# Seven block products instead of eight in the projections of the second 1024 tokens

## The chip, the cores and the metric

The kernel runs on one core of a Trainium2 chip. The metric is the device time of one execution in microseconds, as the median of several runs. The engines are TensorE (PE; its weight loads are shown apart as PEld), VectorE (DVE), ScalarE (ACT), GpSimd (POOL) and SyncE (SP), which issues nearly all transfers.

## The reference

One layer on x of 2048 tokens by 1024. `xn = RMSNorm(x)`, `proj = xn @ w_in`, and `proj` is split into the queries, keys, values and gates of two mixers (qa, ka, va, ga of 512 columns each; qb, gb of 512; kb, vb of 64), an indexer (iq, ik, iw) and two merge gates (za, zb of 1024 each). Mixer A is chunked attention with a relative bias, mixer B attends to the 256 keys per query that the indexer scores highest. Then

```python
merged = gate_a * (ya @ w_branch_a) + gate_b * (yb @ w_branch_b)
h = h + merged @ w_out
return rms_norm(h, final_norm_gain)
```

All data are float32. The change concerns only `xn @ w_in` for the columns qa, ka, ga, qb, gb, za and zb, and the tokens 1024 to 2047.

## The kernel before, in words

**Products.** Each float32 operand is split into a high part, rounded to TensorE's float32 format, and a low part, the rest. `mm3` (line 194) forms a product of 128 by 128 by 512 with three matmuls: high by high, high by low, low by high. The normalized input stands in `xh` and `xl` (lines 150, 151), two slots of [128, 8, 512]: 8 slices of 128 input features, 512 tokens.

**Projections.** `UNITS` (line 63) lists 20 units of 256 columns: zb 4, za 4, gb 2, ga 2, qb 2, va 2, ka 2, qa 2. `steps` (lines 714 to 718) is the order of work: all units on token groups 0 and 1 (the first 1024 tokens), where the last two units go on to groups 2 and 3, then the other units on groups 2 and 3. `prep` (line 173) loads and splits one unit's weights (ScalarE the high part, GpSimd the low part), one unit ahead, in two buffers; each unit's weights are loaded once for each pass. The main loop (line 1177) runs each step: two column tiles of 8 x 3 = 24 matmuls of 512 columns (for va, token tiles of 24 matmuls of 288 columns), each into one of three PSUM banks, and `evac` (line 665) applies the gate's function or the split and stores the result to DRAM. `norm_again` (line 1167) replaces the input of groups 0 and 1 by that of groups 2 and 3 in the same slots.

**What runs beside it.** After each column tile the loop calls `tick(1)` (line 1152; 0.5 for va). While the indexer's scores (`logits`, line 442) and the search for the 256 best keys (`search`, line 477) have work left, a tick lets them put `PUMP` = 3850 ns of counted work into the program (`pump`, line 622). Once they are done and `OPEN` = 138 ticks have passed (of 160), `open_early` (line 731) closes the search's memory, and each tick puts two rounds of attention (`attention`, line 1122) into the program, up to a pause before the seventh unit. After the projections the attention goes on, followed by the output product.

**Order.** The source gives each instruction a priority by its place in the program; a planner then lays down, ahead of time, a fixed order for every engine and for the SP queue: of the instructions that it takes to be ready, the earliest in the program first. On the chip each engine runs its list in that order. Tiles of a pool with one tag share its buffers, so a write waits for the last reader of the tile before.

## Time and profile before

| | us |
|---|---|
| median of 3 runs | 2084.61 (2083.42 to 2085.93) |
| profiled execution | 2085.01 |
| its span, first to last instruction | 2083.2 |

The profile shows one execution. A busy time is the time in which an engine had at least one instruction under way; matmuls are pipelined, so the time from start to start in a full stretch, not the duration of one, tells what a matmul costs. The times on the left of rows are counted from the start of the span.

### The profile page before, as it was taken

How to read it: one execution, taken by the hardware profiler on the slowest of the kernel's cores; microseconds unless marked ns; L12 is line 12 of the kernel's file. 1: busy time of each engine (PE TensorE's matmuls, PEld its weight loads, DVE VectorE, ACT ScalarE, POOL GpSimd, SP SyncE). 2: the span in 40 equal slices, each digit the busy share in tenths (PEclk: the TensorE clock that was granted, in tenths of full speed). 3: DMA queues.
4: the chain of work that ended last, by engine and by line, in shares of the span. 5: the costliest groups of instructions: out<-in, count | busy, mean ns of one | idle time of the engine just before them, and what ended most of it. 6: DMA issues, size and time to landing. Idle time of an engine off the chain costs nothing. (4 is left out here: it accounts for less than half of the span.)

```text
span 2083.2 us, 33122 instructions
## 1 busy us (share of the span) xinstructions
PE 2023.5 (97%) x10858; PEld 1719.6 (83%) x10858; DVE 1316.1 (63%) x3380; ACT 1196.3 (57%) x2372; POOL 688.3 (33%) x753
## 2 busy tenths in 40 slices
PE   8799999999999999999999999999999999999998
PEld 7578887889888888887987888888898888887886
DVE  6747958786987845002325668766885688865444
ACT  5455655555456454223436778866896698873221
POOL 2122223221202211122323455445444644442410
PEclk9899999999999999999999999999999999999999
DMA  9473344464443333226557774666346632145642
GB/s 354 155 223 117 134 143 143 139 205 146 157 170 137 117 112 105 86 91 197 186 185 224 222 215 148 180 189 207 114 136 190 215 119 65 62 137 187 213 141 91
DMA packets 237378, 331.12 MB, mean 159 GB/s; under 512 B 29328, under 2 KB 119824, under 8 KB 237072
## 3 DMA queue, kind: packets, MB, share of 16 engines
q1 hardware_dynamic: 237200, 328.96, 48.9%
q8 instruction: 86, 1.41, 0.3%
q14 instruction: 92, 0.75, 0.1%
HBM read 222.47 MB, written 106.40 MB: 158 GB/s over the span
## 5 line engine op out<-in xcount | busy, mean ns | idle before, releaser
L199 PE MATMUL acc<-xh,wt 128*128 128x512 f32 x2304 | 738.8, 395 | 2.6 <-DVE e L318 2.6
L199 PEld LDWEIGHTS acc<-xh,wt 128*128 128x128 f32 x2304 | 431.9, 188 | 101.1 <-DVE e L318 2.8
L199 PE MATMUL acc<-xl,wt 128*128 128x512 f32 x1152 | 452.9, 393 | 0.0
L191 POOL TENSOR_TENSOR wt<-wst,wt 128x512 fp32r<-128x512 f32 (+1 forms) x172 | 202.2, 1192 | 634.1 <-ACT wt L190 625.1
L199 PEld LDWEIGHTS acc<-xl,wt 128*128 128x128 f32 x1152 | 216.7, 188 | 48.8
L807 POOL TENSOR_TENSOR ptl<-pf,pth 128x512 fp32r<-128x512 f32 (+1 forms) x144 | 179.4, 1246 | 214.9 <-ACT pf L803 157.5
L467 DVE SCALAR_TENSOR_TENSOR sc<-lg,iw,sc 128x512 f32<-128x512 f32 (+2 forms) x266 | 179.2, 680 | 81.0 <-ACT lg L462 72.1
L810 DVE TENSOR_TENSOR ptl<-pt,pth 128x512 fp32r<-128x512 f32 (+1 forms) x288 | 187.5, 660 | 53.0 <-ACT pth L809 51.8
L965 PE MATMUL s<-kBt,qsB 128*128 128x512 f32 (+3 forms) x640 | 188.3, 384 | 2.3 <-issue 2.0
L462 ACT ACTIVATE lg<-lg 128x512 f32<-128x512 f32 (+2 forms) x304 | 150.9, 525 | 53.5 <-PE lg L460 52.4
L809 ACT ACTIVATE pth<-pt 128x512 fp32r<-128x512 f32 (+1 forms) x288 | 161.2, 579 | 27.4 <-PE pt L982 13.8
L982 PE MATMUL pt<-ident,P 128*128 128x128 f32 x1088 | 167.1, 273 | 2.1 <-DVE ptl L810 0.8
L968 ACT ACTIVATE P<-P,mx 128x128 f32<-128x128 f32 (+15 forms) x128 | 154.6, 1209 | 18.2 <-DVE mx L786 17.5
L990 PE MATMUL O<-pth,vBt 128*128 128x256 f32 x544 | 148.1, 290 | 2.1 <-DVE yb L1000 1.5
L990 PE MATMUL O<-ptl,vBt 128*128 128x256 f32 x544 | 147.2, 296 | 1.6 <-POOL ptl L807 1.1
L786 DVE CUSTOM_DVE_ANT_0 P<-s,mk,mx 128x512 f32<-128x512 f32 (+2 forms) x192 | 125.2, 652 | 34.3 <-PE s L965 28.3
L190 ACT ACTIVATE wt<-wst 128x512 fp32r<-128x512 f32 (+1 forms) x172 | 92.7, 575 | 81.0 <-DMA wst<-wP 78.5
L982 PEld LDWEIGHTS pt<-ident,P 128*128 128x128 f32 x1088 | 128.4, 140 | 11.4 <-ACT pf L803 2.1
L1028 POOL TENSOR_TENSOR dw<-dst,dw 128x512 fp32r<-128x512 f32 x64 | 82.6, 1291 | 116.2 <-ACT dw L1027 102.1
L965 PEld LDWEIGHTS s<-kBt,qsB 128*128 128x128 f32 x640 | 103.1, 191 | 14.8 <-DVE mx L786 5.1
L990 PEld LDWEIGHTS O<-pth,vBt 128*128 128x128 f32 x544 | 102.9, 189 | 10.7 <-ACT pth L809 2.4
L860 ACT ACTIVATE P<-P,mx 128x640 f32<-128x640 f32 (+4 forms) x128 | 98.1, 767 | 23.2 <-DVE mx L786 22.7
(247 smaller groups left out, 3958.1 us busy)
## 6 DMA issues: line engine op xcount, KB each, us to landing
wst<-wP SPq DMA_DIRECT2D x132, 256.0 KB
qs<-qA SPq DMA_DIRECT2D x128, 128.0 KB
kk<-kA SPq DMA_DIRECT2D x56, 256.0 KB
vs<-vA SPq DMA_DIRECT2D x56, 256.0 KB
bias<-biasD SPq DMA_DIRECT2D x32, 320.0 KB
xrow<-x SPq DMA_DIRECT2D x16, 512.0 KB
sBD<-ef SPq DMA_DIRECT2D x32, 256.0 KB
sAD<-ef SPq DMA_DIRECT2D x32, 256.0 KB
```

The lines of the kernel that those rows point to most:

```text
L191: nc.gpsimd.tensor_tensor(wt[:, 1, k:k + n, c * 128:(c + 1) * 128], st, f32(hi), op=OP.subtract)
L199: nc.tensor.matmul(acc, a, b, start=(i == 0), stop=(i == n - 1))
L462: nc.scalar.activation(lg, lg, AF.Relu)
L467: nc.vector.scalar_tensor_tensor(o_, lg, wv, o_, op0=OP.mult, op1=OP.add)
L786: nc.vector.tensor_tensor_reduce(dst, ps_, add, 1.0, FMAX if first else mx, OP.add, OP.min, accum_out=mx)
L807: nc.gpsimd.tensor_tensor(lo, pf, f32(hi), op=OP.subtract)
L809: nc.scalar.activation(hi, src, AF.Copy)
L810: nc.vector.tensor_tensor(lo, src, f32(hi), op=OP.subtract)
L965: nc.tensor.matmul(s_ps[:, :w], q[:, h, :], kBt[:, m, a:a + w], start=(m == 0), stop=(m == 1))
L968: nc.scalar.activation(P[:, e, :n], P[:, e, :n], AF.Exp, bias=mx[:, e:e + 1], scale=-1.0, accum_out=st["sum"][:, (u % 2) * 2 + e:(u % 2) * ...
L982: nc.tensor.transpose(pt[:, k, e, :], P[:, e, (kt + k) * 128:(kt + k + 1) * 128], ident)
L990: nc.tensor.matmul(o_, vBt[:, kt + k, :], src[:, k, :], start=(kt + k == 0 and n_ == 0), stop=(kt + k == b and n_ == 1), skip_group_check= ...
```

## The change

For 18 units (all but va) the second pass takes the 1024 tokens as two blocks of 512 (groups 2 and 3), the 1024 input features as two blocks of 512 (`A11`, `A12` of group 2, `A21`, `A22` of group 3), and a unit's 256 columns as two of 128. The eight block products are replaced by seven of 4 x 3 = 12 matmuls, by Strassen's scheme, with block sums of the input (in place of the old blocks) and of the weights.

The work is cut in two halves over all units. In the first (`prep_one`, `first_half`), each unit does four products with A11, A21 (by then A11 - A21), A12 and A22 (as loaded), evacuates one finished block, and stores three partial sums to DRAM (`qD`). Between the halves `combine_pe` forms two more block sums on TensorE, with plus or minus the identity as weights; the first and the last sum use `combine` (GpSimd, VectorE, ScalarE). In the second half (`prep_two`, `load_sums`, `part`) each unit does the other three products, adds the sums that it loads from DRAM, and evacuates three blocks. A unit's weights are loaded whole for the first half and three quarters for the second, in rows of 512 bytes; the block sums of weights are made on GpSimd (`TPE`) and their low parts on VectorE (`LOE`). The input block A11 and the first half's weights give up their memory to the second half's weights and sums. The units go in the order `QUADS`. The constants `OPEN` and `PUMP` change; a product of the new kind counts half a tick, so that the program has 151 ticks in place of 160. The order of the last steps of the first pass is turned (group 1 before 0, and 3 before 2), so that group 3 is in place first.

In `evac` the last buffer can be given by the caller (`own`, the sum's own tile), and for qb the two half operations come before the whole one. The core of the diff:

```diff
-OPEN = 138
+OPEN = 142
...
-PUMP = 3850
+PUMP = 4300
...
+QUADS = "qb zb zb qb zb zb ka za za za za ka gb gb qa ga ga qa"
+QB, CTB, WSB = 1, 2, 5
+W2AT = (2, 0)
+TPE, LOE = "gpsimd", "vector"
...
+    qD = [scratch(f"qD{u}", [3, 128, 512]) for u in range(len(UNITS))]
...
+    a_st = phase_p.enter_context(ExitStack())
+    apool = a_st.enter_context(pool("xA"))
+    parts = {(s, h, z): (apool if s + h == 0 else xpool).tile([128, 4, 512], F32R, name=f"x{z}{s}{h}")
+             for s in range(2) for h in range(2) for z in "hl"}
...
+    def mm3(acc, pairs, first=True, last=True):
...
-    steps = [(u, g) for u in range(nu - 2) for g in (0, 1)]
-    steps += [(a_, 0), (b_, 0), (a_, 1), (b_, 1), (a_, 2), (b_, 2), (a_, 3), (b_, 3)]
-    kinds = ("zb", "za", "gb", "ga", "qb", "va", "ka")
-    second = [u for k in kinds for u in range(nu - 2) if UNITS[u][0] == k]
-    steps += [(u, g) for u in second for g in (2, 3)]
-    runs = list(range(nu)) + second
-    last = {}
-    for i, (u, g) in enumerate(steps):
-        last[u if i < 2 * nu + 4 else nu + second.index(u)] = i
+    of = {k: [u for u in range(nu) if UNITS[u][0] == k] for k in dict(UNITS)}
+    va = of["va"]
+    left = {k: list(of[k]) for k in of}
+    quads = [left[k].pop(0) for k in QUADS.split()]
+    rest = []
+    jobs = [("std", u, u, g) for u in range(nu - 2) for g in (0, 1)]
+    jobs += [("std", u, u, g) for g in (1, 0) for u in (a_, b_)]
+    jobs += [("std", nu + u, u, g) for u in rest for g in (3, 2)]
+    jobs += [("std", nu + u, u, g) for g in (3, 2) for u in va]
+    turned = max(i for i, j_ in enumerate(jobs) if j_[3] == 3)
+    jobs += [("one", 2 * nu + u, u, 0) for u in quads]
+    runs = list(dict.fromkeys(j_[1] for j_ in jobs))
...
+    def combine(dst, a, b, op, k):
+        (ah, al), (bh, bl), (dh, dl) = a(k), b(k), dst(k)
+        t, t2 = (evl.tile([128, 512], F32, name="ct", tag="ct", bufs=CTB) for _ in range(2))
+        nc.gpsimd.tensor_tensor(t, f32(ah), f32(bh), op=op)
+        nc.vector.tensor_tensor(t2, f32(al), f32(bl), op=op)
+        nc.vector.tensor_tensor(t, t, t2, op=OP.add)
+        nc.scalar.activation(dh, t, AF.Copy)
+        nc.vector.tensor_tensor(dl, t, f32(dh), op=OP.subtract)
...
+    def combine_pe(dst, a, b, z, k, free):
+        n = (count_["acc"] + 1 + (k % 2 if free == 2 else 0)) % 3
+        acc = (psp, psp, psz)[n].tile([128, 512], F32, name="cm", tag=f"acc{n}")
+        for i, (w, x_) in enumerate(((0, a(k)[0]), (0, a(k)[1]), (z, b(k)[0]), (z, b(k)[1]))):
+            nc.tensor.matmul(acc, signs(w), x_, start=(i == 0), stop=(i == 3))
+        dh, dl = dst(k)
+        nc.scalar.activation(dh, acc, AF.Copy)
+        nc.vector.tensor_tensor(dl, acc, f32(dh), op=OP.subtract)
...
+    def split_w(W, st, k):
+        nc.scalar.activation(W[:, 0, :, k], st, AF.Copy)
+        getattr(nc, LOE).tensor_tensor(W[:, 1, :, k], st, f32(W[:, 0, :, k]), op=OP.subtract)
+    def prep_one(u, at):
+        wt = wpool.tile([128, 2, KT, WT], F32R, name="wt", tag="wt")
+        W = blocks_of(wt, 4)
+        e = getattr(nc, TPE)
+        for k in range(4):
+            st = evl.tile([128, 4, 128], F32, name="wst", tag="wst", bufs=stage[-1][2])
+            for c in range(2):
+                nc.sync.dma_start(st[:, 2 * c:2 * c + 2], io["wP"][u, c, :, k::4, :])
+            e.tensor_tensor(st[:, 2], st[:, 3], st[:, 2], op=OP.subtract)
+            e.tensor_tensor(st[:, 3], st[:, 2], st[:, 0], op=OP.add)
+            e.tensor_tensor(st[:, 3], st[:, 1], st[:, 3], op=OP.subtract)
+            split_w(W, st, k)
+        wcur[at] = W
+    def product(acc, W, b, x_, first, last):
+        mm3(acc, [((W[:, 0, b, k], W[:, 1, b, k]), x_(k)) for k in range(4)], first, last)
+    def first_half(u, W):
         kind, c2 = UNITS[u]
+        a, b = next_acc(5), next_acc(5)
+        p1, s, d = (evl.tile([128, 512], F32, name=f"q{z}", tag=f"q{z}", bufs=QB) for z in range(3))
+        product(a, W, 0, A11, True, False)
+        nc.scalar.activation(p1, a, AF.Copy)
+        nc.sync.dma_start(qD[u][0], p1)
+        yield
+        product(b, W, 2, A21, True, False)
+        nc.vector.tensor_tensor(s, b, p1, op=OP.add)
+        nc.sync.dma_start(qD[u][1], s)
+        yield
+        product(a, W, 1, A12, False, True)
+        evac(kind, c2 * 2, 2, a)
+        yield
+        product(b, W, 3, A22, False, True)
+        nc.vector.tensor_tensor(d, b, p1, op=OP.add)
+        nc.sync.dma_start(qD[u][2], d)
+        yield
...
+    for i, (how, r_, u, g) in enumerate(jobs):
+        kind, c2 = UNITS[u]
+        wt, s_ = wcur[r_], SLOT[g]
+        if how == "one":
+            for n, _ in enumerate(first_half(u, wt)):
+                if u == quads[-1] and n == 1:
+                    for k in range(4):
+                        combine_pe(A21, A22, A21, 1, k, 1)
+                tick(0.5)
...
+        if i == turned:
+            again += [lambda k=k: combine(A21, A11, A21, OP.subtract, k) for k in range(4)]
...
+    w_st.close()
+    second = {}
+    def prep_two(q):
+        u = quads[q]
+        wt = w2.tile([128, 2, 3, 4, 128], F32R, name="wt2", tag="wt2", bufs=3)
+        W = [wt[:, :, z] for z in range(3)]
+        e = getattr(nc, TPE)
+        for k in range(4):
+            if (q, k) < W2AT:
+                st = evl.tile([128, 4, 128], F32, name="wst", tag="wst", bufs=stage[-1][2])[:, 0:3]
+            else:
+                st = w2.tile([128, 3, 128], F32, name="wst2", tag="wst2", bufs=4)
+            nc.sync.dma_start(st[:, 0:1], io["wP"][u, 0, :, k:k + 1, :])
+            nc.sync.dma_start(st[:, 1:3], io["wP"][u, 1, :, k::4, :])
+            e.tensor_tensor(st[:, 1], st[:, 1], st[:, 0], op=OP.subtract)
+            e.tensor_tensor(st[:, 0], st[:, 2], st[:, 1], op=OP.subtract)
+            split_w(wt, st, k)
+        second.setdefault(q, [None, None, None])[0] = W
+    def load_sums(q):
+        second.setdefault(q, [None, None, None])[1] = [w2.tile([128, 512], F32R, name="part", tag=f"p{z}", bufs=2) for z in range(3)]
+        for z in range(3):
+            nc.sync.dma_start(f32(second[q][1][z]), qD[quads[q]][(2, 1, 0)[z]])
+    def part(q, z):
+        u = quads[q]
+        kind, c2 = UNITS[u]
+        W, sums, acc = second[q]
+        if z == 0:
+            acc = second[q][2] = next_acc(5)
+        mm3(acc, [((W[z][:, 0, k], W[z][:, 1, k]), (A21, A22, A12)[z](k)) for k in range(4)], z == 0, z == 2)
+        s = sums[z]
+        nc.vector.tensor_tensor(f32(s), acc, f32(s), op=OP.add)
+        evac(kind, c2 * 2 + (z > 0), 2 if z == 2 else 3, f32(s), own=s)
+        tick(0.5)
+    nq = len(quads)
+    for k in range(4):
+        combine_pe(A22, A21, A11, 0, k, 2)
+    a_st.close()
+    w2 = phase_p.enter_context(pool("w2"))
+    for q in range(2):
+        load_sums(q)
+    for q in range(2):
+        prep_two(q)
+    part(0, 0)
+    for k in range(4):
+        combine(A12, A12, A21, OP.subtract, k)
+    for q in range(nq + 1):
+        if q < nq:
+            if q + 2 < nq:
+                prep_two(q + 2)
+            if q:
+                part(q, 0)
+        if q:
+            part(q - 1, 2)
+            if 1 < q + 1 < nq:
+                load_sums(q + 1)
+        if q < nq:
+            part(q, 1)
```

## Rows read from the trace of the kernel before

**Rows 1.** The page's engine line, and three lines of its 40 equal slices (52 us each; busy share in tenths; DMA is the share of the 16 DMA engines):

```profile
PE 2023.5 (97%) x10858; PEld 1719.6 (83%) x10858; DVE 1316.1 (63%) x3380; ACT 1196.3 (57%) x2372; POOL 688.3 (33%) x753
...
PE   8799999999999999999999999999999999999998
...
DVE  6747958786987845002325668766885688865444
...
DMA  9473344464443333226557774666346632145642
```

**Rows 2.** Stretches of the second pass of the projections and of what follows it. Columns: from:to, length, then busy us (and instructions) of PE, PEld, DVE, ACT and POOL, the granted clock, the DMA share and GB/s; the stretch 950 to 1010 lies within 930 to 1105:

```profile
640.00:830.00 190.00, 190.00 (x823) 154.07 (x822) 128.21 (x301) 103.92 (x158) 46.67 (x36) 1.00 0.35 122
830.00:930.00 100.00, 100.00 (x433) 81.05 (x432) 0.00 (x0) 21.13 (x37) 20.34 (x16) 1.00 0.26 90
930.00:1105.00 175.00, 166.57 (x938) 145.56 (x937) 50.73 (x136) 65.15 (x175) 47.51 (x53) 0.99 0.58 180
950.00:1010.00 60.00, 52.45 (x301) 44.89 (x300) 16.23 (x47) 26.25 (x71) 19.36 (x24) 1.00 0.74 225
1105.00:1120.00 15.00, 11.59 (x66) 9.65 (x65) 7.32 (x28) 10.04 (x28) 4.83 (x5) 0.87 0.87 258
```

**Rows 3.** The same columns for a stretch of 50 us in which TensorE runs projection matmuls alone:

```profile
850.00:900.00 50.00, 50.00 (x218) 40.50 (x217) 0.00 (x0) 9.57 (x17) 10.18 (x8) 1.00 0.27 91
```

**Rows 4.** Groups of equal instructions: line, engine, operation, out<-in, shapes, count, then busy us and mean ns of one, then the idle time of the engine before them and what ended it:

```profile
L199 PE MATMUL acc<-xh,wt 128*128 128x512 f32 x2304 | 738.8, 395 | 2.6 <-DVE e L318 2.6
L199 PE MATMUL acc<-xl,wt 128*128 128x512 f32 x1152 | 452.9, 393 | 0.0
...
L191 POOL TENSOR_TENSOR wt<-wst,wt 128x512 fp32r<-128x512 f32 x132 | 171.8, 1321 | 547.4 <-ACT wt L190 543.7 <-ACT vv L702 2.8 <-DMA wst<-wP 0.8
...
L190 ACT ACTIVATE wt<-wst 128x512 fp32r<-128x512 f32 x132 | 76.7, 624 | 53.7 <-DMA wst<-wP 53.6
...
L676 ACT ACTIVATE ef<-acc,bm 128x512 f32<-128x512 f32 x64 | 43.7, 683 | 96.5 <-PE acc L199 59.7 <-issue 31.4 <-DMA sAD<-ef 4.3
...
L191 POOL TENSOR_TENSOR wt<-wst,wt 128x256 fp32r<-128x256 f32 x40 | 30.4, 768 | 86.8 <-ACT wt L190 81.4 <-ACT vvt L702 2.7 <-DMA wst<-wP 2.4
...
L1263 DVE TENSOR_TENSOR hh<-po,xr 128x512 f32<-128x512 f32 x32 | 22.0, 689 | 65.7 <-PE po L1242 64.4 <-issue 1.3
L695 DVE SCALAR_TENSOR_TENSOR el<-acc,eh 128x512 fp32r<-128x512 f32 x31 | 21.2, 685 | 7.1 <-ACT eh L694 7.1
...
L1010 DVE TENSOR_TENSOR sgB<-pt,sgB 128x256 f32<-128x256 f32 x32 | 13.4, 419 | 1.2 <-PE pt L1007 1.1
...
L670 ACT ACTIVATE ef<-acc 128x512 f32<-128x512 f32 x32 | 19.1, 596 | 75.0 <-PE acc L199 57.5 <-issue 17.2
...
L212 DVE TENSOR_TENSOR xl<-xs,xh 128x512 fp32r<-128x512 f32 x16 | 10.5, 682 | 0.0
```

**Rows 5.** VectorE's groups by line, those of the indexer's scores and of the top-k search (lines 465 to 559), costliest first: the first two and the last of 42, whose busy times add up to 514 us:

```profile
L467 DVE SCALAR_TENSOR_TENSOR sc<-lg,iw,sc 128x512 f32<-128x512 f32 (+2 forms) x266 | 179.2, 680 | 81.0 <-ACT lg L462 72.1 <-DVE sc L467 0.5
L518 DVE TENSOR_SCALAR_CACHE_REDUCE jk<-sc,st 128x384 bf16<-128x384 f32 (+6 forms) x49 | 63.6, 1298 | 1.5
...
L559 DVE DVE_READ_ACCUMULATOR bad<-bad 128x1 f32 x1 | 0.1, 76 | 0.0
```

**Rows 6.** Two lines of the code with their spread. Columns: line, engine, operation, out<-in, count, then minimum/median/maximum duration in ns, first and last start in us, shapes. The first is a VectorE subtraction with both inputs in SBUF, at the end of the kernel; the second is GpSimd's weight subtraction:

```profile
L1086 DVE TENSOR_TENSOR wosl<-ost,wosh x6: 680/686/1344, 1800.4 to 1844.7; 128x512 fp32r<-128x512 f32 x6
...
L1086 DVE TENSOR_TENSOR wosy<-ost,wosy x4: 691/802/1753, 1865.7 to 1881.3; 128x512 fp32r<-128x512 f32 x4
...
L191 POOL TENSOR_TENSOR wt<-wst,wt x172: 722/1292/2952, 49.4 to 1069.2; 128x512 fp32r<-128x512 f32 x132, 128x256 fp32r<-128x256 f32 x40
```

**Rows 7.** The DMA queues in three stretches, 900 to 950, 1700 to 1720 and 1110 to 1120 us, in this order: packets by size, and what the data queue's packets took as a share of 16 engines' time:

```profile
DMA packets 2436, 4.50 MB, mean 90 GB/s; under 512 B 256, under 2 KB 256, under 8 KB 2432
...
q1 hardware_dynamic: 2432, 4.46, 26.0%
...
DMA packets 1700, 1.16 MB, mean 58 GB/s; under 512 B 95, under 2 KB 1493, under 8 KB 1698
...
q1 hardware_dynamic: 1698, 1.14, 21.0%
...
DMA packets 3454, 3.28 MB, mean 328 GB/s; under 512 B 191, under 2 KB 2430, under 8 KB 3454
...
q1 hardware_dynamic: 3454, 3.28, 109.3%
```

**Rows 8.** The issue of a weight load by the SP queue, minimum/median/maximum in ns:

```profile
L188 SPq DMA_DIRECT2D wst<-wP x172: 327/333/1516, 36.2 to 1065.5; - x172
```

**Rows 9.** The stretch 930 to 1105 us again, projection matmuls (line 199) alone: PE and PEld busy us (instructions), granted clock, DMA share, GB/s:

```profile
930.00:1105.00 175.00, 148.15 (x760) 123.36 (x759) 0.99 0.58 180
```

**Rows 10.** TensorE in order of time in the same stretch: start us, us, instruction, count, and in brackets the idle time before it with what ended it:

```profile
959.84 0.71 PE L855 MATMUL s<-kk,qs 128*128 128x128 f32 x4 [1.21 <-DMA kk<-kA]
...
972.46 0.33 PE L890 MATMUL pt<-ident,P 128*128 128x128 f32 x1 [1.17 <-ACT P L860]
```

79 lines of the change are left out of this document (53 added, 26 removed).

## Prediction

> **What bounds the kernel now.** I read the page first: TensorE is busy 97% of the span, and 9 tenths in every slice but the first two and the last, while no other engine is above 63% [rows 1]. So a saving has to take work from TensorE's queue, or remove idle time from it. The stage table shows where the changed work lies: the second pass of the projections (tokens 1024 to 2047) runs from about 640 to 1105 us, with TensorE full from 640 to 930 and 8.4 us short of full from 930 to 1105, where the first attention units are woven in [rows 2]. In 850 to 900 us nothing but projection matmuls runs: 218 of them in 50.00 us, 229.4 ns from one 512-column matmul to the next [rows 3]; the mean of 395 ns in the groups is a pipelined duration and is not used for sums. VectorE is busy 128 of 190 us until 830, and not at all from 850 to 900: the top-k search has ended by then [rows 2, 3]. The reader should see that this stage is bound by the number of matmuls, and that its other engines and its DMA queue (35% of capacity until 830, 26% after) have room [rows 2, 3].
>
> **The matmuls.** There are 18 units of 256 columns beside the two of kind "va". Each now costs 2 token groups x 2 column tiles x 24 = 96 matmuls of 512 columns in the second pass; seven block products of 12 make 84. That removes 18 x 12 = 216. Two of the block sums are made on TensorE: 8 calls of four matmuls, 32 more. Net 184 x 229.4 ns = **42.2 us less**. All of it lies on the path, because the engine has no idle time there to absorb it. What the change adds lies on other engines, and costs only where TensorE comes to wait. There are four such places.
>
> **First half (18 units, 48 matmuls = 11.0 us each).** Per unit VectorE gets four 128x512 subtractions for the weights' low parts (GpSimd did them before) at 0.68 and two additions out of PSUM at 0.69, 4.1 us; GpSimd gets twelve 128x128 operations in place of four of 128x512: 1.32 at 512 and 0.77 at 256 columns give an estimated 0.49 each, 5.9 us [rows 4]. ScalarE's four conversions stay, and one copy of 0.6 comes. None of this fills 11.0 us alone, but VectorE also still carries the indexer's scores and the search: the costs that the code gives their steps add up to 511 us, and their 42 groups were busy 514 us [rows 5], so one counted unit is one microsecond. The new rate of 4300 ns per tick uses 88 x 4.3 = 378 us before the first half begins (tick 88) and spends the other 133 us by tick 119, thus over 15.5 units. There VectorE has 133 + 15.5 x 4.1 = 197 us to do in 15.5 x 11.0 = 171 us of matmuls plus some 5 us of indexer matmuls: 21 us too much. The cover: three PSUM banks let TensorE run about three products (8 us) past a late addition, and the search may slip, since it has to be done only at tick 142. But each search step is earlier in program order than the additions behind it, and ScalarE's copy and VectorE's sum must be out of a bank one product (2.75 us) after its end. Queued behind a late addition are the other product on that bank, and the store on SP's queue.
> A subtraction with both inputs in SBUF takes 0.68 us in the usual case, and up to 1.75 while GpSimd works; GpSimd's weight subtraction is 1.29 in the median and 2.95 at most [rows 6]. With GpSimd busy half of the time, four such subtractions lose about 4 x 0.5 x 0.25 = 0.5 us per unit, 7 us in all. Bounds 0 and 28; I take **8**, nearer the lower end because the search chain leaves gaps while it waits for ScalarE.
> The Trainium skill (SBUF — State Buffer, section "SBUF: two separate sides") says that a VectorE operation with two SBUF inputs and a GpSimd operation that reads SBUF exclude each other for the whole instruction. The stretched durations agree with it; where the lock never met, this term would be 7 us smaller at its upper end.
>
> **Between the halves.** Four block sums go through one PSUM bank: 4 matmuls 0.92, ScalarE 0.6, VectorE 0.68, about 2.2 us per slice, 8.8 for four; the last slice of the next sum 0.9; then the first weights of the second half 1.1, because their tiles lie where the old block and the old weights were. That is 10.8 us, beside 5.5 us of products and 7.3 us of the sums' own matmuls. VectorE has about 20 us to do until the third product (eight halves of sums, eight 384-column splits at an estimated 0.55 between 0.42 at 256 and 0.68 at 512 columns, and twelve operations of the last sum) where TensorE has 21 [rows 4]. Bounds 0 and 13; I take **4** for signals between engines.
>
> **Second half (18 units, 36 matmuls = 8.26 us each, 149 us).** Here the DMA queue decides. Per unit it loads 0.75 MB of weights again in 1536 pieces of 512 B, loads three sums (384 pieces of 2 KB) and stores three results (384, or 768 for q and k kinds). A 2 KB packet took 0.260 x 50 x 16 / 2176 = 95 ns from 900 to 950 us; from 1700 to 1720, with 205 such taken off, 1398 packets of mostly 512 B took 34 ns each [rows 7]. That is (1536 x 34 + 768 x 95)/16 = 7.8 us for twelve units and 10.1 us for six, 154 us together. From 1110 to 1120 the same mix ran at 109% of counted time and 328 GB/s [rows 7], by which it is 141 us. From tick 142, the last 18 products, the loads of five attention units come on the same queue, 1.5 MB each, 23 us; TensorE gets about 8 us of attention there. So the queue needs 164 to 177 us beside 157 us of TensorE. Weights are three units ahead and sums two, which hides latency but not a lack of rate. SP issues 14 to 17 transfers of 0.33 us per unit [rows 8], 5 to 6 of 8.26 us, in order, each store waiting for ScalarE or VectorE with the next loads behind it. VectorE (2.2 + 2.1 us per unit), ScalarE (about 4) and GpSimd (eight operations, 3.9) have room. Bounds 0 and 20, and more if packets slow down (a rival below); I take **9**.
> The Trainium skill (DMA: Bandwidth & Descriptors, section "Specifications") gives 512 B as the size from which a transfer runs at line rate. The rows disagree: 512 B at the 2 KB rate would be 24 ns, not 34. By the rule the half would need 138 us of queue time instead of 154, this term would be near 0 and the sum about 2060.
>
> **Attention that loses its cover.** Counted in the code, the kernel before weaves 38 rounds of attention (up to the pause) beneath its last 22 ticks; the new one has 9 ticks, 18 rounds. From 930 to 1105 us TensorE was busy 166.6 us, 148.2 of it projections [rows 2, 9], so these rounds are 18.4 us of TensorE; 20/38 of them, 9.7 us, now follow the projections. From 1105 to 1120, where two such units run nearly alone, TensorE is busy 11.6 of 15 us [rows 2]; at that share 9.7 us cost 2.9 of idle; at a full 7 us per unit for 3.5 units they cost 15. Against it, some of the 7.5 us idle from 950 to 1010, which are waits of woven rounds for a load or an exponential [rows 2, 10], goes. Bounds -4 and 15; I take **5**. The rest (order of ka and qa, an earlier search in the first pass, evacuations moved in place) is hidden by TensorE's full queue, as evacuation is now; without that cover it would be one 0.69 us operation per bank.
>
> **Sum.** -42.2 + 8 + 4 + 9 + 5 = -16.2. The profiled execution took 2085.0 us (span 2083.2) and the median of the runs is 2084.6, so the forecast is 2084.6 - 16.2 = **2068 us**.
>
> **Rivals.**
> - *Nearly everything is kept.* Every new wait finds cover: the four terms together cost 0 to 12 us, giving 2043 to 2056, about 2050. For it: VectorE, ScalarE and GpSimd are each far from full in the stage [rows 2]; against it: the queue's demand in the second half. Chance 0.24.
> - *VectorE sets the pace of the first half.* The 21 us of excess demand and the waits on GpSimd come through, about 20 instead of 8 us: 2080, within 2077 to 2086. For it: the search's steps come first on an in-order engine; against it: banks and slack until tick 142. Chance 0.12.
> - *The DMA queue sets the pace of the second half, and the kernel is slower.* One mechanism: 18 x 1536 small loads among stores. With the other terms as above the gain is gone and 4 us lost when the half takes 29 us more than TensorE needs, 157 + 29 = 186 us of queue time; the upper bound is 177, and each nanosecond on a 512 B packet adds 1.7 us, so it decides from about 40 ns per packet. At 45 ns it gives about 2099, within 2089 to 2107. For it: no stretch of the profile sustains such a rate for over 50 us except the first, with larger packets [rows 1]; against it: 328 GB/s in the same mix. Chance 0.18.
>
> **How the numbers follow.** Forecast 0.46 (its own range 2056 to 2080), then 0.24, 0.12 and 0.18. The range leaves out a fifth: the faster third of the first rival and the worse half of the last, 2047 to 2095. A difference under 0.2% (4 us) is about what a measurement of this kernel can't tell from none. Faster: 0.46 + 0.24 + 0.01 = 0.71; same 0.11; slower 0.18.
>
> **What would show it.** In the profile after: 216 fewer 512-column projection matmuls and 32 new ones of the block sums; the first half at 11.0 us per unit without gaps (right), or gaps before second products that VectorE's sum ended (second rival); between the halves one gap of a few us; in the second half a DMA share near 100% and waits of TensorE for weight splits or sums that a load ended (third rival), or a full TensorE at a share under 90% (first rival); after the projections, a short stretch of attention alone with TensorE about 8 tenths busy. The prediction fails if the static order that the planner lays down lets TensorE run into waits in places not named here.

## The result, and the profile after

The changed kernel takes 2098.9 us (median of 4 runs, 2098.6 to 2104.2) where the kernel before takes 2084.0 on the same chip: ratio **1.0077** (95% interval 1.0059 to 1.0096), some 16 us slower. The forecast was 16 us faster. Three executions of over 2400 us, among those of the experiments, are left out of all ratios.

The page of the changed kernel, the lines that answer to [rows 1]:

```profile
PE 2000.5 (95%) x10674; PEld 1687.6 (80%) x10674; DVE 1479.2 (71%) x3646; ACT 1267.2 (60%) x2484; POOL 804.8 (38%) x1043
...
PE   8799999999999999999888999999999999999998
...
DMA  9473345364464665478889764556346632145642
```

TensorE has the 184 matmuls less that were counted (10858 to 10674), but it is busy only 23 us less and idle 37 us more. Its row of nines has a hole at slices 20 to 22, 996 to 1153 us, and the DMA row stands at 7 to 9 from slice 18 to 23, 891 to 1206 us. The stage table, with the columns of [rows 2]; first half, passage, second half in two parts, and what follows:

```profile
655.00:873.00 218.00, 212.65 (x955) 173.92 (x955) 167.46 (x364) 103.76 (x175) 110.22 (x211) 0.99 0.60 198
873.00:897.00 24.00, 19.27 (x71) 13.55 (x70) 19.58 (x28) 9.75 (x18) 5.14 (x4) 0.93 0.28 98
897.00:1030.00 133.00, 119.50 (x485) 91.02 (x483) 70.81 (x113) 55.03 (x96) 56.80 (x110) 0.97 0.83 262
1030.00:1097.00 67.00, 58.11 (x264) 44.42 (x265) 34.96 (x81) 49.41 (x92) 20.87 (x32) 0.95 0.87 274
1097.00:1200.00 103.00, 90.52 (x515) 75.15 (x514) 63.87 (x202) 77.58 (x207) 49.41 (x55) 0.95 0.88 243
```

At the rate of [rows 3], 4.36 matmuls per us, 133 us hold 580; here they hold 485, although the PE column says 119.5 us busy. So read the count, not the busy time: a matmul whose next weights come late is shown as longer. Two lines bound the halves, ScalarE's copy of a unit's first product (18 of them, first half) and VectorE's addition of a sum (54, second half):

```profile
L1274 ACT ACTIVATE q<-acc x18: 571/579/615, 672.1 to 871.5; 128x512 f32<-128x512 f32 x18
...
L1367 DVE TENSOR_TENSOR part<-acc,part x54: 651/691/693, 897.6 to 1094.3; 128x512 f32<-128x512 f32 x54
```

From the first copy to the last lie 17 units of 11.0 us and about 3.4 us of indexer matmuls (15, at the same rate): 190.6 needed, 199.4 taken, **8.8 lost**. From the last copy to the first addition lie 36 + 32 + 12 matmuls, 18.3 us: 26.1 taken, **7.8 lost**. From the first addition to the last lie 53 products, 145.9 us, and the woven attention, 8.7 by the forecast: 196.7 taken, **42 lost**. The forecast had 8, 4 and 9. "Lost" is counted against a TensorE that never waits, and the woven attention at its TensorE time alone. What TensorE waited for in the second half (897 to 1097; line waited for, us, times, longest), and then its weight load's first line:

```profile
PE acc L218 <- ACT wt L1248: 10.8, 13, 2.5
PE pt L915 <- ACT P L885: 4.1, 5, 1.4
PE s L880 <- DVE mx L811: 3.2, 3, 1.5
```

```profile
PEld acc L218 <- ACT wt L1248: 17.1, 17, 3.0
```

The weights' splits are late. The chain behind them, from 897 to 1097: ScalarE's splits waited 48.8 us for GpSimd's block sums, GpSimd's 60.8 us for the loads. Who holds the loads? The DMA engines are 83% busy, and SyncE looks like this (start, duration, issue; six weight loads among four stores):

```profile
937.60 0.38 SPq L1347 DMA_DIRECT2D wst<-wP  x1
938.03 0.48 SPq L719 DMA_DIRECT2D qB<-part  x1
938.56 0.55 SPq L1348 DMA_DIRECT2D wst<-wP  x1
939.21 0.54 SPq L1347 DMA_DIRECT2D wst<-wP  x1
939.80 0.55 SPq L1348 DMA_DIRECT2D wst<-wP  x1
940.45 0.54 SPq L1347 DMA_DIRECT2D wst<-wP  x1
941.03 0.55 SPq L1348 DMA_DIRECT2D wst<-wP  x1
941.68 0.54 SPq L698 DMA_DIRECT2D sBD<-part  x1
942.32 0.38 SPq L719 DMA_DIRECT2D qB<-eh  x1
942.79 1.43 SPq L719 DMA_DIRECT2D qB<-part  x1
```

In these rows SyncE has no pause beyond some 0.1 us between two issues. In the 133 us from 897 to 1030 it made 204 (107 weight loads, 33 sum loads, 49 stores, 15 for attention): they took 103 us together, 0.51 each, and the pauses of over 0.2 us add up to 16 us, five of them over 1 us. So SyncE is nearly full, though not without waits of its own. That made the first theory.

### The profile page after: what moved, and what is told of

It reads as the page before. It is cut to its first block, busy times and chain, and to the rows that moved or that the text cites. A ratio compares the mean times of both kernels' runs of the same rounds, so it can differ in the third digit from the quotient of the medians.

```text
span 2096.8 us, 34363 instructions
## 1 busy us (share of the span) xinstructions
PE 2000.5 (95%) x10674; PEld 1687.6 (80%) x10674; DVE 1479.2 (71%) x3646; ACT 1267.2 (60%) x2484; POOL 804.8 (38%) x1043
## 4 chain that ended last, share of the span: by engine, by line
PE 43%; DMA 7%; ACT 3%; DVE 3%; issue 2%; POOL 2%; SPq 1%; DVEq 0%; POOLq 0%; ACTq 0%
PE po L1432 8%; PE d L218 7%; PE O L1015 6%; PE s L990 5%; PE pt L1007 5%; PE acc L218 4%; PE O L925 3%; PE pt L915 2%; PE s L880 2%; DMA wst<-wP 2%; DMA dst<-wB 1%; DMA dst<-wA 1%; DVE P L811 1%; DMA bias<-biasD 0%; DMA sg<-gAD 0%
## 5 line engine op out<-in xcount | busy, mean ns | idle before, releaser
L218 PE MATMUL acc<-xh,wt 128*128 128x512 f32 x2160 | 700.2, 397 | 22.9 <-ACT wt L1248 12.3
L218 PEld LDWEIGHTS acc<-xh,wt 128*128 128x128 f32 x2160 | 405.5, 189 | 126.3 <-ACT wt L1248 19.2
L218 PE MATMUL acc<-xl,wt 128*128 128x512 f32 x1080 | 425.1, 394 | 0.0
L218 PEld LDWEIGHTS acc<-xl,wt 128*128 128x128 f32 x1080 | 204.2, 189 | 43.2
L210 POOL TENSOR_TENSOR wt<-wst,wt 128x512 fp32r<-128x512 f32 (+1 forms) x92 | 118.0, 1309 | 270.3 <-ACT wt L209 241.7
L1248 ACT ACTIVATE wt<-wst 128x512 fp32r<-128x512 f32 (+1 forms) x144 | 76.4, 571 | 94.2 <-POOL wst L1350 48.8
L1249 DVE TENSOR_TENSOR wt<-wst,wt 128x512 fp32r<-128x512 f32 (+1 forms) x144 | 95.2, 684 | 48.7 <-ACT wt L1248 43.1
L880 PE MATMUL s<-kk,qs 128*128 128x320 f32 (+1 forms) x448 | 108.3, 339 | 7.5 <-DVE mx L811 4.6
L218 PE MATMUL d<-ya,dw 128*128 128x512 f32 x384 | 108.2, 407 | 6.2 <-ACT dw L1052 5.8
```

Source lines behind the costliest of these rows:

```text
L218: nc.tensor.matmul(acc, a, b, start=(first and i == 0), stop=(last and i == n - 1), **({} if first and last else {"skip_group_check": True}))
L880: nc.tensor.matmul(s_ps[:, :w], q[:, m, j * 128:(j + 1) * 128], kk[:, ko:ko + w], start=(m == 0), stop=(m == 1))
```

## The experiments

**Theory: SyncE's issuing paces the second half.** Rivals: the DMA engines' capacity (the packet size of the forecast's last rival), and the staging and compute chain behind the loads. Ratios below are to the kernel before, on the same chip; 0.001 is 2.1 us.

**1. Half as many weight loads in the second half.** A copy of the weights, reordered so that a k's blocks are neighbours:

```diff
-            nc.sync.dma_start(st[:, 0:1], io["wP"][u, 0, :, k:k + 1, :])
-            nc.sync.dma_start(st[:, 1:3], io["wP"][u, 1, :, k::4, :])
+            nc.sync.dma_start(st[:, 0:3], io["wQ"][u, k, :, 1:4, :])
```

> Second half only: the three weight blocks of one k lie side by side in DRAM (a reordered copy of the same weights), so one load of 128 rows of 1.5 KB takes the place of two loads with 384 pieces of 512 B. Same bytes; 72 loads in place of 144. Theory (SyncE's issuing paces the second half: 15 to 16 issues in every 10 us from 895 to 1025, about 0.62 us each with their gap): a unit's weight issues fall from 8, about 4.7 us, to 4, about 1.8 to 2.6 us; a unit then has 10 to 13 issues, 6 to 8 us, beside 8.26 us of TensorE, so the weights come in time. Second half 165 to 175 in place of 200 us, time about 2070 (2062 to 2078). Rival A (the DMA queue's capacity, 512 B packets too slow): 1536 pieces at about 30 ns become 512 at about 72 ns, 0.6 us less queue time per unit, 11 us in all: 2085 to 2092. Rival B (staging of four tiles and the chain GpSimd, ScalarE, VectorE behind each load): that chain stays as it is, 2093 to 2099.

Measured: **1.0009** (0.9996 to 1.0022), 14 us off the changed kernel, about 2086 by the ratio. That is short of the theory's range and inside rival A's (packet size), so this run alone doesn't decide between them.

**2. The same number of loads, but the old packets** (64 unused columns behind every 128 in DRAM):

```diff
+            nc.sync.dma_start(st[:, 0:3], io["wQ"][u, k, :, 1:4, 0:128])
```

> As the wide load, but with 256 B of unused space behind every 512 B block in DRAM, so that one load still consists of 384 pieces of 512 B: half as many loads, the same packets as in the changed kernel. Theory (SyncE's issuing paces): if an issue costs by the number of loads, as fast as the wide one, about 2070; if it costs by the pieces (0.33 us were seen for 128, 0.55 for 256), a load takes about 0.77 us, a unit saves 4 x (0.43 + 0.55 + 0.2 - 0.77 - 0.1) = 1.2 us, and the time is 2078 to 2088. Rival A (packet size and queue capacity): no gain, 2096 to 2101. Rival B (staging and the compute chain): no gain, 2096 to 2101.

Measured: **1.0010** (0.9994 to 1.0025), the same. The stage rows 897 to 1030 of the wide and then the padded version, each followed by the packets of that stretch:

```profile
897.00:1030.00 133.00, 123.33 (x513) 96.59 (x512) 72.88 (x121) 57.86 (x103) 57.64 (x110) 0.97 0.85 273
```

```profile
DMA packets 22608, 36.34 MB, mean 273 GB/s; under 512 B 2494, under 2 KB 10465, under 8 KB 22598
```

```profile
897.00:1030.00 133.00, 121.15 (x498) 93.97 (x498) 71.54 (x120) 56.73 (x101) 57.43 (x110) 0.97 0.87 264
```

```profile
DMA packets 35465, 35.15 MB, mean 264 GB/s; under 512 B 2412, under 2 KB 23702, under 8 KB 35456
```

Rival A expected no gain here. So what was won came from the number of issues; 13,000 packets more in this stretch cost nothing that the times show. But only 14 of the expected 30 us came: in the wide version TensorE still waited 8.5 us for splits from 897 to 1097, with SyncE no longer full (156 issues in 64 of the 133 us).

**3. Stores issued by ScalarE** in place of SyncE, loads as they were.

```diff
-            nc.sync.dma_start((sAD if kind == "za" else sBD)[g][rows], e)
+            (nc.scalar if own is not None else nc.sync).dma_start((sAD if kind == "za" else sBD)[g][rows], e)
```

> Second half only: the stores of a unit's results are issued by ScalarE's own queue in place of SyncE's: 3 to 6 of a unit's 14 to 17 issues, and with them SyncE's waits for ScalarE and VectorE; the same transfers, bytes and packets. Theory (SyncE's issuing paces): 4 issues x 0.62 = 2.5 us per unit less on SyncE, the units' rest of 11 issues is 6.8 us: second half 165 to 180 us, time 2070 to 2082, unless ScalarE (some 4 us of 8.26 per unit) becomes late with its splits by its new issues of about 0.4 us each. Rival A (queue capacity): the transfers are the same, 2095 to 2103. Rival B (staging and the compute chain): ScalarE is in that chain and gets more to do, 2099 to 2106.

Measured: 1.0038 (1.0023 to 1.0054), 8 us off. The same bytes on the same engines in fewer issues on SyncE: for the theory, though less than half of what it expected. The stores' own waits left SyncE with them, so the run doesn't test the number of issues alone. SyncE made 152 issues from 897 to 1030, about as few as in the wide version, and waited 27 us instead for landed stores ahead of a sum load:

```profile
SPq L1357 <- DMA sBD<-part: 9.4, 4, 2.8
...
SPq L1357 <- DMA sAD<-part: 6.8, 5, 2.8
SPq L1357 <- DMA kA<-part: 6.0, 2, 3.3
SPq L1357 <- DMA qB<-part: 5.1, 2, 3.9
```

In the changed kernel these waits were 8 us.

**4. No sum loads.**

> Leaves out the loads of the partial sums from DRAM from the third unit of the second half on (the additions use what the tiles hold): 48 loads of 256 KB, 12.6 of the 53 MB of the second half. Theory (SyncE's issuing paces): 3 issues of 14 to 17, 1.9 us per unit less: the issues that are left (11 to 14, 6.8 to 8.7 us) are near TensorE's 8.26, the time 2072 to 2085. Rival A (queue capacity): 24% of the queue's work goes; the half falls to what TensorE needs, 2062 to 2072. Rival B (compute chain): only the additions' waits for these loads go (5.7 us on VectorE), 2093 to 2099.

Measured: 0.9938 (0.9915 to 0.9962), 29 us off, with GpSimd's, ScalarE's and VectorE's chain unchanged (the kernel leaves out the sums, so its results are not the layer's). That chain is not the bound. At 2072 us by this ratio it lies where the ranges of the theory and of capacity meet, and doesn't tell them apart.

**Second theory.** In the wide version SyncE waited 36 us for the same thing, 897 to 1030:

```profile
SPq L1356 <- DMA sBD<-part: 14.9, 11, 2.5
SPq L1356 <- DMA sAD<-part: 14.7, 7, 3.2
SPq L1347 <- DVE wt L1249: 8.3, 13, 2.0
SPq L1356 <- DMA kA<-part: 6.0, 4, 2.7
```

Line 1356 loads a sum into the tile from which a result was just stored, and waits for that store to land; weight loads stand behind it. Two remedies of order, each alone on the wide version, and two runs on attention. First, results in tiles of their own:

```diff
-        evac(kind, c2 * 2 + (z > 0), 2 if z == 2 else 3, f32(s), own=s)
+        evac(kind, c2 * 2 + (z > 0), 2 if z == 2 else 3, f32(s))
```

> The wide weight loads of the second half, and a unit's result is written to the small evacuation tiles (two of them) in place of the tile of its partial sum; so the load of the next sum into that tile waits for ScalarE's or VectorE's read and no longer for the store of the result to land. In the wide version SyncE waited 37 of 133 us (897 to 1030) for such stores ahead of a sum load, with weight loads in the queue behind. Theory now (SyncE's in-order queue is late with the weight loads, first by the number of its issues, then by its waits): the waits before weight loads go, TensorE's 8.5 us of waits and some 10 us of stretched weight loads in the half shrink to a few: 12 us off the wide version's 2088, about 2076 (2070 to 2082). Rival (the DMA engines are the bound, 85% busy and bursty): the queue's work is the same, 2085 to 2091. Second rival (two evacuation tiles are too few, ScalarE now waits for the stores in SyncE's place): 2088 to 2097.

Measured: 1.0022 (1.0008 to 1.0037), no gain; 3 us above the wide version, within the error. By its profile the theory and the second rival were both right, in different stretches; first 897 to 1030 and 1030 to 1097, then ScalarE's waits in the latter:

```profile
897.00:1030.00 133.00, 127.41 (x534) 100.22 (x533) 74.69 (x131) 64.45 (x118) 61.63 (x117) 0.96 0.89 294
1030.00:1097.00 67.00, 56.94 (x252) 44.98 (x251) 32.25 (x69) 48.39 (x88) 21.45 (x29) 0.87 0.79 241
```

```profile
ACT ef L691 <- DMA qA<-eht: 5.6, 2, 4.0
ACT eht L715 <- DMA qA<-elt: 2.4, 2, 1.7
ACT eht L715 <- DMA gAD<-ef: 1.6, 1, 1.6
```

Until 1030 there are 534 matmuls in place of 513, and the waits for splits in the half fell from 8.5 to 2.2 us; after it, when the code puts the high and low parts of the last results into the two evacuation tiles as well, ScalarE waits for stores instead (252 matmuls in place of 288). TensorE's granted clock is lower there too, 0.87 where the wide version had 0.96, which over 67 us is 6 us at most; the run doesn't separate the two.

Second, the sum loads behind the next weight loads:

```diff
             if q + 2 < nq:
                 prep_two(q + 2)
+            if q > 1:
+                load_sums(q)
             if q:
                 part(q, 0)
...
-            if 1 < q + 1 < nq:
-                load_sums(q + 1)
```

> The wide weight loads, and a unit's three sum loads are placed one step later in program order, behind the next weight loads, just ahead of the first product that needs them. Theory (SyncE's waits for landed stores ahead of a sum load hold back the weight loads): weight loads go first, weights are in time, the half gets 5 to 12 us shorter, 2076 to 2083; but the sums come later, VectorE's additions may wait 1 to 2 us per unit for them. Rival (DMA engines are the bound): 2085 to 2091. Second rival (late sums hold the banks): 2090 to 2105.

Measured: 0.9996 (0.9984 to 1.0007): 3 us, within the error and below what was expected.

Attention (`OPEN = 142` becomes 999, then 126):

> The wide weight loads, and no attention unit is begun before the projections end (tick 142 becomes 999). It measures what the nine woven ticks are worth and takes their loads (1.5 MB for each unit) out of the second half. If the DMA engines bind the last third of the half (96 to 100% busy from 1030 to 1097 in the wide version), that third is freed of a third of its bytes and gets about 15 us shorter, of which 8 to 9 are attention work that only moves: the time is 2080 to 2090. If attention needs the projections' matmuls as cover, 18 rounds with 8.7 us of TensorE follow later at 77% and the next stretch has lost its cover too: 2092 to 2102.

Measured: 1.0043 (1.0026 to 1.0060), 7 us slower than with woven rounds. Attention needs that cover: what follows the last addition takes 28.6 us more (1028.9 in place of 1000.3). But its price in the half is high as well: the additions take 161.9 us in place of 183.5, so 18 woven rounds cost 21.6 us and not the 8.7 of their TensorE time.

> The wide weight loads, and attention opens at tick 126 in place of 142, so that 25 ticks, up to the whole 38 rounds, are woven into the second half as in the kernel before. If the gap to the forecast is lost cover (22 us that the stretch after the projections is longer than before), the time falls by 5 to 12 us to 2076 to 2083. If the DMA engines (or SyncE's queue) bind the half, 3.5 more units with 1.5 MB and 12 issues each come on them, 16 us of queue time and 26 us of SyncE, and the projections end later by about what attention gains: 2084 to 2100.

Measured: 1.0036 (1.0021 to 1.0051), 6 us slower. Earlier attention lengthens the half (last addition at 1109.6 in place of 1082.9) by more than it shortens what follows (990.5 in place of 1000.3 us), so the late opening is not where the forecast's gain went.

**The remedies together.** wide_mixed keeps separate result tiles only until attention opens (`own=s if early_ else None`); both_mixed has the wide loads in the first half too (`nc.sync.dma_start(st, io["wQ"][u, k])`, the blocks' places exchanged in the arithmetic); both_mixed_order has the sum loads behind the weight loads as well.

> The wide weight loads of the second half; results go to evacuation tiles of their own only until the attention pools open, and into the sum's tile after that. In the run with separate tiles throughout, TensorE's waits for weight splits fell (8.5 to 2.2 us in the half) and 897 to 1030 held 534 matmuls in place of 513, but from 1030 ScalarE waited 9.6 us for stores out of the two tiles, which attention's results then share. Theory (weight loads held back on SyncE behind sum loads that wait for landed stores): the gain of the first two thirds is kept, 21 matmuls or 5 us, and the loss of the last third goes: 0.9975 to 0.9995 of the kernel before, about 2082. Rival (the DMA engines are the bound; what the first thirds win the last gives back): 1.0005 to 1.0025, as the wide version or worse.

Measured: 0.9987 (0.9971 to 1.0002), as expected.

> As wide_mixed, and the first half's four blocks of one k come by one load of 2 KB rows too, in place of two with 512 pieces of 512 B: 72 issues less on SyncE, 36,864 packets in place of 9,216 become 9,216. Theory (SyncE and the queue are not the bound of the first half: 11 issues in 11 us, DMA 60% busy, TensorE idle 5.3 of 218 us, for VectorE's split and ScalarE's copy): at most 3 us less than wide_mixed. Rival (the weights of the first half are late for the loads too): 5 to 9 us less, all that the first half lost.

(Packets of the first half: 36,864 become 9,216.) Measured: **0.9951** (0.9935 to 0.9967), 7.5 us less than wide_mixed: the rival.

> As both_mixed, and the sum loads are placed behind the next weight loads in program order. Alone, beside the wide loads, this order measured 0.9996 against 1.0009. Theory (both remedies serve the same wait, SyncE's for landed stores ahead of a weight load): nothing to 3 us less than both_mixed, about 0.997 to 0.999 of the kernel before. If they serve different waits the gains add, 0.9955 to 0.9975.

Measured: **0.9905** (0.9890 to 0.9920), 20 us faster than the kernel before and 36 us faster than the changed one. That is below both ranges expected: beside the wide loads the later sum loads alone had brought 3 us, here they bring 10. Its first half and its stretch 897 to 1030, then the data queue in that stretch, then the additions:

```profile
655.00:873.00 218.00, 215.04 (x974) 177.18 (x973) 166.23 (x366) 105.22 (x177) 104.54 (x212) 0.99 0.60 200
...
897.00:1030.00 133.00, 128.17 (x563) 102.99 (x562) 76.35 (x141) 72.00 (x135) 65.91 (x123) 0.99 0.93 308
```

```profile
q1 hardware_dynamic: 25411, 40.76, 92.3%
```

```profile
L1365 DVE TENSOR_TENSOR part<-acc,part x54: 671/682/692, 895.0 to 1066.1; 128x512 f32<-128x512 f32 x54
```

The DMA engines move 308 GB/s for 133 us where the changed kernel moved 262, and the second half's additions take 171 us in place of 197. TensorE's waits for weight splits from 897 to 1030 fell from 10.3 to 1.6 us. GpSimd's waits for loads did not fall (49.6 us before the remedies, 61.9 with them): an engine that is early waits as long as one that is starved, so only TensorE's own waits tell whether weights are late.

**What is left without any supply.**

> Leaves out, in the second half, all weight loads with their block sums and splits from the fourth unit on and all sum loads from the third (weights and sums of earlier units are used again): TensorE's matmuls, VectorE's additions, the evacuation, the stores and attention stay. It shows what the whole supply of the second half costs, and what is left of the forecast's miss outside it. Theory (the second half's supply costs 42 of the 56 us that the change lost of its 42 us saving and its cover): the second half near its 157 us of TensorE, 160 to 168 in place of 197 to 200: 2058 to 2068. If attention's own waits and the lower clock after gaps are the larger part, 2070 to 2080 (the run without sum loads alone measured 0.9938).

Measured: 0.9875 (0.9861 to 0.9890), 26.0 us faster than before, at the fast end of what was expected. The additions, and the stretch 897 to 1030:

```profile
L1373 DVE TENSOR_TENSOR part<-acc,part x54: 651/692/692, 900.1 to 1063.7; 128x512 f32<-128x512 f32 x54
```

```profile
897.00:1030.00 133.00, 130.83 (x576) 107.28 (x575) 53.54 (x90) 50.02 (x80) 9.62 (x15) 0.99 0.48 163
```

**Which remedy needs which?** Four more runs:

> The changed kernel with its narrow loads (two per k and half, 512 B pieces) and the two remedies of order alone: separate result tiles until attention opens, sum loads behind the weight loads. Theory (the number of issues is the first limit, 15 to 16 per 10 us; order matters only once it is lifted): little, 1.002 to 1.007 of the kernel before. Rival (the order on SyncE's queue, loads behind waits for landed stores, is the whole cause): 0.992 to 0.999, most of the way to the run with all remedies (0.9905).

Measured: 1.0067 (1.0045 to 1.0089), as expected. With the old number of issues both remedies of order bring 2 us, within the error.

> The changed kernel with one wide load per k in both halves, and neither remedy of order. With the wide loads in the second half alone it measured 1.0009. Theory (first-half weights are late too, by 7 us): 0.996 to 0.998. Rival (the first half gained only together with the remedies of order, or by chance): 0.9995 to 1.002.

Measured: 0.9974 (0.9958 to 0.9989), 7 us below the wide version: the first half's part is its own.

> Everything as in the fastest version so far except the first half, which keeps its two loads of 512 B pieces per k. If the first half's gain is its own (7 us, as between wide_mixed and both_mixed), 0.993 to 0.995; if the order of the sum loads gains only together with separate result tiles and the first half does not matter to it, the same; if the later order gained because the first half ended differently, 0.997 to 1.000.

Measured: 0.9929 (0.9905 to 0.9952), as for a part of the first half that is its own (5 us here, within the error).

> The fastest version so far with 256 B of unused space behind every 512 B block of the reordered weights: the same number of loads, but 512 B pieces in both halves, 1.8 times the packets of weights. Theory (the number of issues counts and not the packets): 0.990 to 0.994, within 0.3% of 0.9905. Rival (the size of packets matters once the issues are few and the queue is 93% busy): 0.994 to 1.000; 55,000 more packets in the two halves at 28 ns for 512 B, less what the wide ones took, are some 0.7 us of queue time per unit, 12 us in each half.

Measured: 0.9922 (0.9902 to 0.9942), within the error of 0.9905 although there are 46,000 more packets (72 loads with 384 more, and 72 with 256 more: 18,432 packets of weights become 64,512; the expectation's 55,000 and its factor of 1.8 are wrong).

| weight loads | order as changed | both remedies of order |
|---|---|---|
| two per k, both halves | 1.0077 | 1.0067 |
| one per k in the second half | 1.0009 | 0.9929 |
| one per k in both | 0.9974 | 0.9905 |
| one per k in both, 512 B pieces | not run | 0.9922 |

Down the left column the number of issues alone is worth 21 us. Across, the order is worth 2 us while SyncE is nearly full, and 17 and 14 us once it isn't. SyncE's waits agree: a queue full of issues comes late to a sum load, when the store ahead has mostly landed (8 us of such waits in the changed kernel's stretch 897 to 1030), and an emptier one comes early and stands (27 us in run 3, 36 in the wide version).

## Why the prediction was wrong

**Where the miss lies.** The last projection matmul, before and after:

```profile
L199 PE MATMUL acc<-xh,wt x2304: 387/394/499, 100.0 to 1105.8; 128*128 128x512 f32 x192
```

```profile
L218 PE MATMUL acc<-xh,wt x2160: 387/392/796, 100.1 to 1093.8; 128*128 128x512 f32 x197
```

By these profiled executions the changed kernel is 12.0 us faster up to there and takes 25.6 us more behind it (1003.0 in place of 977.4). The forecast had 30.9 faster (-42.2 - 9.7 of attention moved out + 8 + 4 + 9) and 14.7 slower (9.7 + 5). So 19 of the 30 us of the miss lie in the projections and 11 behind them. The losses below sum to more than 19, since the kernel before lost time in its second pass too (8.4 us idle from 930 to 1105 alone, [rows 2]).

**Matmuls (-42.2): right.** 184 fewer, at about the same rate where TensorE was fed (576 in 133 us without supply, 4.33 per us).

**First half (8, bounds 0 to 28): size right, cause in part another.** 8.8 us were lost, and not only to VectorE's demand and its lock with GpSimd. One load in place of two won 5 to 7.5 us of time with VectorE's and GpSimd's work as it was; by the count above the half then lost 4.7 us (wide loads in both halves, old order) and 5.6 (fastest version) in place of 8.8. So 3 to 4 us of it were late weights; where the rest of the won time lies is open. What remains is nearer to the forecast: from 672 to 872 the fastest version's TensorE waits 2.1 us for ScalarE's copy and 0.9 for VectorE's addition. SyncE issues about 11 transfers in 10 us there and isn't full; which wait on it held the weights was not tried. (The term's 0.5 us per unit make 9 us in 18 units and not 7.) The rival "VectorE sets the pace" had 20 us here; VectorE was busy 167 of 218 us.

**Between the halves (4, bounds 0 to 13): 7.8,** within its bounds. The lower clock is in it (the columns of [rows 2]):

```profile
879.00:883.00 4.00, 3.09 (x13) 2.00 (x12) 2.34 (x4) 0.60 (x1) 1.28 (x1) 1.00 0.42 156
883.00:887.00 4.00, 2.45 (x10) 1.39 (x8) 3.83 (x6) 2.31 (x4) 1.28 (x1) 1.00 0.00 0
887.00:889.00 2.00, 1.37 (x4) 0.90 (x4) 1.45 (x3) 0.51 (x1) 0.40 (x1) 0.72 0.00 0
889.00:891.00 2.00, 2.00 (x6) 1.25 (x4) 1.63 (x2) 0.71 (x2) 0.88 (x1) 0.50 0.00 0
891.00:893.00 2.00, 1.46 (x5) 0.67 (x4) 2.00 (x4) 0.97 (x2) 0.00 (x0) 0.93 0.00 0
```

From 879 to 887 TensorE was busy 5.5 of 8 us, waiting for parts of the block sums; then it was granted half its clock (0.50, 1.2 of 2.4 GHz) for some 3.4 us. The mean of 0.93 over the 24 us of the passage makes that 1.7 of the 7.8 us at most.

**Second half (9, bounds 0 to 20, "and more if packets slow down"): the step that failed.** 42 us were lost. The forecast said "Here the DMA queue decides" and gave SyncE 14 to 17 transfers of 0.33 us, 5 to 6 of 8.26 us per unit, from [rows 8]. That price belongs to a load of 128 pieces on a queue with pauses; the new loads, of 128 and of 256 pieces, took this long (minimum/median/maximum in ns):

```profile
L1347 SPq DMA_DIRECT2D wst<-wP x72: 333/539/616, 855.9 to 1065.6; - x72
...
L1348 SPq DMA_DIRECT2D wst<-wP x72: 545/551/1525, 856.5 to 1066.2; - x72
```

With the 0.51 us that the 204 issues took on average and some 0.07 between two, 14 to 17 of them need 8.1 to 9.9 us per unit before any wait: as much as TensorE's 8.26 or more. The Trainium skill (Perfetto Trace Analysis, section "What "DMA-bound" means") tells apart a kernel bound on DMA engines and one bound on the sequencer that issues, whose track is then solid. The trace agrees in the main: SyncE issued during 103 of the 133 us and paused for 16, while the engines stand at 83%. The page adds that large descriptors help in either case; runs 1 and 2 differ from it, since fewer loads with the same small pieces helped as much. The second error in the step was "weights are three units ahead and sums two, which hides latency": it does not where loads stand in one queue behind a wait for a landed store (36 us of waits in the wide version's rows above, and 17 and 14 us of time in the table).

Not all of the 42 us is supply. Without any supply the additions still take 163.6 us, so the supply cost 33 of them; the remedies of the second half alone (fewer loads, both remedies of order) brought the time down by 31 us (1.0077 to 0.9929). The other 9 are probably the woven rounds, which the count takes at 8.7 us; no run without both shows it. At most 7 of the 42 are TensorE's lower granted clock (mean 0.965 over these 197 us); with wide loads and both remedies of order it was 1.00 (first half narrow) and 0.99 (fastest version), so it came back as the waits went.

**Attention (5, bounds -4 to 15): not confirmed.** What follows the projections takes 25.6 us more where the forecast had 14.7, and no remedy shortened it by more than 5 us: without any supply of the second half it is 1002.8 us. In the half a woven round costs more than twice its TensorE time (21.6 us for 18 rounds in the wide version). Against that stands what the kernel before lost to its 20 further woven rounds, which no run measures, so the net of the term is open. With the second half's supply left out, the other terms were forecast at -42.2 + 8 + 4 + 5 = -25.2 us, and -26.0 was measured; that is partly luck, since even there the additions took 163.6 us where 154.6 were needed, and that version's profiled execution, the slowest of its four, was only 18 us shorter than the one of the kernel before. Opening attention earlier or later made it worse.

**The rivals.** The last one gave "about 2099" and the measured time is 2098.9, but by accident. Its mechanism was packets of 45 ns, from 40 ns on. The changed kernel's queue, 897 to 1030:

```profile
DMA packets 36404, 34.84 MB, mean 262 GB/s; under 512 B 3256, under 2 KB 24888, under 8 KB 36393
...
q1 hardware_dynamic: 36393, 34.72, 82.9%
```

Its packets took 82.9% of 16 x 133 us, 1764 us; less 11,505 of 2 KB at the 95 ns of the prediction, 671 us are left for 21,632 smaller ones, 31 ns each at most, below the 34 that the forecast had taken. Read packet by packet, the trace gives these 28 ns in the mean and 27 in the median. The 34 was misread: in its own stretch, 1700 to 1720 of the kernel before, the 1398 packets took 28 ns in the mean too, and the 205 of 2 KB beside them 132 and not 95. Neither runs 1 and 2 nor the last line of the table shows a price of the size in the time. The fastest version runs at 92% of the queue and 308 GB/s, which the forecast called unproven for so long a stretch. "Nearly everything is kept" (2043 to 2056) was too hopeful: even without any supply of the second half the ratio gives 2059. The fastest version, 0.9905 or 2065 us, is in the forecast's own range.

What stays open: why an issue behind a load of 256 pieces takes longer (last section), how the 14 us of the fewer second-half loads divide between shorter queue and earlier weights, the net price of the moved attention, and whether more staging tiles would help: in the fastest version SyncE's longest wait from 897 to 1030 is a weight load that waits for VectorE to free its tile, 22.6 us in all, and no run changed their number.

## What to carry to other kernels

Count the issues of a queue like work of an engine: number times the duration of such an issue where they stand back to back, plus the gap, against the time that the stage has. Lay out weights so that one load brings what one step needs; here a reordering of the weights and two remedies of order turned a kernel 0.8% slower into one 1% faster. And look at what each load must wait for before it may start, and what is queued behind it: its price shows only when the queue has room, so remedies have to be tried together.

## What was not expected of the hardware

- **An issue's duration is not given by its pieces alone, but also by what was issued before it.** The narrow load of 128 pieces took 0.34 us in the median after a pause of over 0.2 us (7 loads), 0.38 behind a sum load or a store (26) and 0.55 directly behind the load of 256 pieces (39). The wide load of 128 pieces of 1.5 KB took 0.33 after a pause (24) and 0.38 behind another issue (48), the padded one of 384 pieces 0.38 (15) and 0.44 (57). The load of 256 pieces took 0.55 after a pause too, and up to 0.60 in the median behind its like. Why 256 pieces take longer than 384, these runs don't tell. The padded load's row, and then the wide one's:

```profile
L1347 SPq DMA_DIRECT2D wst<-wQ x72: 367/424/1765, 854.0 to 1061.2; - x72
```

```profile
L1347 SPq DMA_DIRECT2D wst<-wQ x72: 328/382/558, 856.7 to 1059.2; - x72
```

- **The DMA engines bore far more than the forecast granted.** 308 GB/s at 93% of the 16 engines over 133 us, most of it in packets of 1.5 and 2 KB, in the fastest version.
- **Small packets cost little more for their bytes:** in the changed kernel from 897 to 1030, 512 B took 27 ns in the median (28 in the mean) and 2 KB 84 (97).
